# Fp32 operands in place of fp16 pairs in the gate products and the filter's second product of a Hyena/RG-LRU block

## The chip, the cores and the metric

The kernel runs on one core of a Trainium2 chip. The metric is the device time of one execution in microseconds (us). The five engines each work through their own instruction stream in order: PE (TensorE, matrix products; its weight loads are shown apart as PEld), DVE (VectorE), ACT (ScalarE), POOL (GpSimd) and SP (SyncE, which issues DMAs). An instruction that waits holds up everything behind it on its engine.

## The reference, cut to what matters

One block of a hybrid backbone over 4096 tokens of width 1024: normalise and modulate, one input projection into 3072 columns, then two groups side by side. The Hyena group is a long convolution by a filter that a small network computes. The RG-LRU group is a bidirectional recurrence with two gates:

```python
def rglru_coeffs(xc, wa, ba, wx, bx, lam):        # wa, wx: 8 heads of 64x64
    r = sigmoid(einsum('blhi,hij->blhj', xh, wa) + ba)     # xh: xc by heads
    i = sigmoid(einsum('blhi,hij->blhj', xh, wx) + bx)
    log_a = -RG_C * r * softplus(-lam)
    a = exp(log_a)
    b = sqrt(-expm1(2.0 * log_a)) * (i * xc)
    return a, b                                  # h[t] = a[t] * h[t-1] + b[t]

def hyena_filter(L, ...):                        # sines of two-layer products, then
    h = (h @ f_w4) * exp(-t * deltas)            # a 64-row product and a decay
    ...                                          # normalised, forward and backward half
def long_conv(u, kernel, bias):
    y = irfft(rfft(u, n=2 * L) * rfft(kernel, n=2 * L), n=2 * L)[:, :L]
```

The outputs of both groups are normalised, gated, joined, projected by `w_out`, added to x and normalised. 256 context tokens go through the projection and the recurrence first; their last states start the recurrence over the 4096 tokens.

## The kernel before, in words

**Precision.** Almost every product is taken as three products of fp16 operands: an fp32 operand is scaled by a power of two, rounded to fp16 (the high half), and the rest is rounded again (the low half); high·high, high·low and low·high are added up in PSUM in fp32. The helpers `mm` and `mms` issue a matmul; every matmul of the trace is recorded on their line, L168. `pow2` and `total` (L175 to L193) work out the power of two from a sum of squares.

**Stages.** From 0 to about 100 us the modulation vectors are formed and the first weights and tokens come in. From 100 to 200 us the context tokens go through (`ctx_in`, L706), while the filter's network (`mlp`) runs. From 200 to about 900 us pass A (`pass_a`, L579) takes 8 blocks i of 512 tokens. For each it runs 12 projections (`inproj`, 24 fp16 matmuls of 128x512 each; weights in tiles named wh and wz, tokens in X), the short convolutions and the forward recurrence of that block (`units_a`, L855, which calls `unit`, L804, with two lanes for each of two pairs of feature blocks). In between go the 64 rows of the filter (`filter_row`, L967, four to a `filter_group`), and the load of the next block's tokens: two additions on POOL per 128 tokens (xt), squares and copies on ACT, a split into halves (xh on ACT, xlo on POOL), transposing DMAs. From 900 to about 1800 us pass B (`blocks_b`, L1024) goes over the blocks backward: the other projections, the backward recurrence (`units_b`, L1092), the FFT stages, the gating. The rest is the inverse transforms and the output projection.

**A unit of the recurrence** (`unit`, L804) is a generator in steps. Step 1 splits xc (128 x 1024, fp32, two feature blocks side by side) into two fp16 halves in the tile xh: a DVE multiplication by a scale (L810) and a DVE multiply-subtract (L811). Step 2: for each lane and each of two gates three fp16 matmuls (L823) into a PSUM tile of 128x512, fa for gate R and fb for gate I, two buffers each, and a sigmoid on ACT from it (L824). Then POOL multiplies I by xc (L460). Step 3: tanh and exp on ACT (L832, L835), a square on POOL. Step 4: DVE (L841), square root on ACT (L842). Step 5: DVE multiplies (L844), the DVE scans (L849) and carry copies (L851). ACT changes its function table (ACT_TABLE_LOAD) when a function of another set comes next: sigmoid, tanh/exp, square root and the filter's exp take turns.

**Preparation of the gates.** `xc_scale` (L744) bounds xc from the weights' sums by some 25 small DVE instructions to get the power of two for the split, with maxima from `xmax` (L401). `gprep` (L767), once for each direction, loads the 128x1024 fp32 gate weights, scales them (L772, DVE), sums squares (L775, ACT), gets the power of two, and splits them into fp16 halves (L778 ACT, L780 DVE).

**A row of the filter** (`filter_row`): a first product (fp16, three matmuls whl x hb into fa), a DVE product with the decay (kd, L975), the split of kd into kh: high half on ACT (L984), low half on POOL (L985); absolute value on ACT (L978) and its sum on POOL (acc, L457). One row later `second` (L989): three fp16 matmuls kh x st1 into fb, a split of the result on ACT (L995) and DVE (L996), and its store. The decay is an exp on ACT (L963), four in advance in the tile dec.

**What sets the order.** The streams are fixed when the program is built, in order of issue in a tile scheduler with priorities. `mms` lets "side" products (gates, filter, FFT) be placed up to SIDE = 64 instructions earlier than they are written, so they stand in among the projections' matmuls. Steps are hung on a counter by `at` and `tick` (L561 to L568), one tick per projection; the tables DC, DA, DS, D0 give each unit's steps their delays (context, pass A, pass B, last block of pass B). PSUM: mm 3 buffers, fa 2, fb 2, sm 1. fa and fb are shared by the gates, the filter and the FFT, and a matmul into a buffer waits until its former contents were read.

Of the kernel before, what the change touches and what calls it, by code (L numbers as in the profile page):

```python
# [28 lines left out]
DC = (1, 2, 4, 5, 5)  # L29
# [29 lines left out]
DA = ((11, 12, 14, 15, 15), (3, 4, 4, 6, 6), (0, 3, 5, 6, 8))  # L59
# [16 lines left out]
def tables():  # L76
# [35 lines left out]
    t["t_s1"] = np.stack([np.concatenate([hi[:64], hi[:64]]), np.concatenate([lo[:64], lo[:64]]), hi, lo])  # L112
# [50 lines left out]
class K:  # L163
# [73 lines left out]
    def consts(self):  # L237
        nc, a, cp = self.nc, self.a, self.cp
        self.ident = cp.tile([128, 128], F32, name="ident")
        nc.scalar.dma_start(self.ident, a["t_id"])  # L240
        self.ones = cp.tile([128, 128], F32, name="ones")
        nc.vector.memset(self.ones, 1.0)
        self.onesb = cp.tile([128, 128], BF16, name="onesb")
        nc.vector.memset(self.onesb, 1.0)
        self.col = cp.tile([128, 110], F32, name="col")
        self.sT = cp.tile([128, 2, 8], F32, name="sT")
        self.usq = cp.tile([128, NB, 8], F32, name="usq")
        self.shl = cp.tile([128, 2, 8, 2], F16, name="shl")
        self.smax = cp.tile([128, 2], F32, name="smax")
# [67 lines left out]
    def mod(self, pool, ml, xp, part):  # L317
# [42 lines left out]
        if part == 1:  # L360
            junk = pool.tile([128, D], F32, name="gr", bufs=1)
            self.s1, self.sx, self.rsx = s1, *self.xscale(junk, s1, 0)
            self.at(1, lambda: self.xmax(junk, 0))
            return
# [35 lines left out]

    def xmax(self, sq, which):  # L401
        self.nc.vector.tensor_reduce(self.smax[:, which:which + 1], sq, axis=AX.X, op=OP.max)
# [176 lines left out]
    def pass_a(self):  # L579
        tc, nc, a = self.tc, self.nc, self.a  # L580
        with ExitStack() as es, ExitStack() as right:
# [69 lines left out]
            for d in (0, 1, 2, 4):  # L651
                self.at(CT + d, lambda: next(ctx))
# [56 lines left out]
    def ctx_in(self, ap, hy, W):  # L709
# [10 lines left out]
        self.xmax(sq, 1)  # L720
        self.xc_scale(rn, W)
        self.gh, self.rg = [None, None], [None, None]
        self.gprep(0, rn)
        yield
# [19 lines left out]
    def xc_scale(self, pool, W):  # L744

        nc = self.nc
        B = pool.tile([128, NB], F32, name="xb0")
        E = pool.tile([128, NB], F32, name="xb1")
        G = pool.tile([128, 16], F32, name="xb2")
        m = pool.tile([128, 1], F32, name="xb3")  # L750
        for j in range(NB):
            nc.vector.tensor_copy(B[:, j:j + 1], W["xr", j][4])
            be = W["xr", j][2]
            nc.vector.tensor_mul(G[:, 0:2], be, be)
            nc.vector.tensor_reduce(E[:, j:j + 1], G[:, 0:2], axis=AX.X, op=OP.add)
        nc.vector.tensor_reduce(m, self.smax, axis=AX.X, op=OP.max)
        nc.vector.tensor_scalar(m, m, 1.01 * D, None, op0=OP.mult)
        nc.vector.scalar_tensor_tensor(B, B, m, E, op0=OP.mult, op1=OP.add)
        nc.vector.tensor_mul(G, self.col[:, 48:64], self.col[:, 48:64])
        nc.vector.tensor_reduce(E, G.rearrange("p (k j) -> p j k", k=4), axis=AX.X, op=OP.add)  # L760
        nc.vector.scalar_tensor_tensor(B, B, 16.0, E, op0=OP.mult, op1=OP.mult)
        nc.vector.tensor_mul(E, self.col[:, 64:68], self.col[:, 64:68])
        nc.vector.scalar_tensor_tensor(B, E, 2.0, B, op0=OP.mult, op1=OP.add)
        nc.vector.tensor_reduce(m, B, axis=AX.X, op=OP.add)
        self.sxr, self.rxr = self.pow2(self.cp, m, 15, 0, "xr", 1)

    def gprep(self, d, pool):  # L767

        nc, a = self.nc, self.a
        gw = self.wp.tile([128, NB, 2, 128], F32, name="wr", bufs=1)  # L770
        nc.sync.dma_start(gw, a["rg_w"][d])
        nc.vector.tensor_scalar(gw, gw, self.rxr, None, op0=OP.mult)  # L772
        gh = pool.tile([128, 2, NB, 2, 128], F16, name=f"gh{d}")
        gq = pool.tile([128, 1], F32, name=f"gq{d}")
        nc.scalar.activation(gh[:, 0], gw, AF.Square, accum_out=gq)  # L775
        t = self.total(pool, self.ps, gq, "g")
        sg, self.rg[d] = self.pow2(pool, t, 15, 0, f"g{d}", 1)
        nc.scalar.activation(gh[:, 0], gw, AF.Copy, scale=sg)  # L778
        f = lambda t: t.rearrange("p j g c -> p (j g c)")
        nc.vector.scalar_tensor_tensor(f(gh[:, 1]), f(gw), sg, f(gh[:, 0]), op0=OP.mult, op1=OP.subtract)  # L780
        self.gh[d] = gh
# [22 lines left out]
    def unit(self, pool, lanes, n, xc, fin, sig=None):  # L804
# [4 lines left out]
        xh = pool.tile([128, 2052], F16, name="xh", bufs=2)  # L809
        nc.vector.tensor_scalar(xh[:, :2 * n], x2, self.sxr, None, op0=OP.mult)  # L810
        nc.vector.scalar_tensor_tensor(xh[:, 1026:1026 + 2 * n], x2, self.sxr, xh[:, :2 * n], op0=OP.mult,  # L811
                                       op1=OP.subtract)
        yield
        R = pool.tile([128, 1026], F32, name="R", bufs=2)
        I = pool.tile([128, 1026], F32, name="I", bufs=2)
        for l, (d, j) in enumerate(lanes):
            for g, dst, bias in ((0, R, 68 + 4 * d + j), (1, I, 76 + 4 * d + j)):
                for q0 in range(0, n, 512):
                    m = min(512, n - q0)
                    c = n * (j % 2) + q0  # L820
                    ps = self.pst("fa" if g == 0 else "fb", 2)
                    for k, (gi, xi) in enumerate(((0, 0), (0, 1), (1, 0))):
                        self.mms(ps[:, :m], self.gh[d][:, gi, j, g, :], xh[:, 1026 * xi + c:1026 * xi + c + m], k == 0, k == 2)  # L823
                    nc.scalar.activation(dst[:, n * l + q0:n * l + q0 + m], ps[:, :m], AF.Sigmoid,  # L824
                                         bias=self.ccol(bias), scale=self.rg[d])
# [12 lines left out]
        M = xh.bitcast(F32)[:, :L * n]  # L838
# [76 lines left out]
    def filter_setup(self, pool):  # L915
        tc, nc, a = self.tc, self.nc, self.a
        self.st1 = pool.tile([128, 256], F16, name="st1")
        nc.scalar.dma_start(self.st1.rearrange("p (h m) -> p h m", h=2), a["t_s1"][2:4].rearrange("h p m -> p h m"))
# [48 lines left out]
    def filter_row(self, pool, n, hb, dec):  # L967
# [6 lines left out]
        kd = pool.tile([128, 512], F32, name="kd", bufs=1)  # L974
# [8 lines left out]
        kh = pool.tile([128, 2, 512], F16, name="kh", bufs=2)  # L983
        nc.scalar.activation(kh[:, 0], kd, AF.Copy)  # L984
        nc.gpsimd.tensor_sub(kh[:, 1], kd, kh[:, 0])  # L985
# [3 lines left out]
        def second():  # L989
            ps = self.pst("fb", 2)  # L990
            for x, (ti, ki) in enumerate(((0, 0), (0, 1), (1, 0))):
                self.mms(ps, self.st1[:, 128 * ti:128 * ti + 128], kh[:, ki, :], x == 0, x == 2)
# [10 lines left out]
    def filter_l1(self, pool, kd):  # L1003
# [10 lines left out]
        br = pool.tile([1, 512], F32, name="kh", bufs=2)  # L1014
# [77 lines left out]
    def units_b(self, rn, i):  # L1092
# [14 lines left out]
        def sig(p):  # L1107
# [4 lines left out]
            return f  # L1112
        us = zip(*[self.unit(rn, [(1, 2 * p), (1, 2 * p + 1)], 512, xcs[p],
                             lambda h, p=p: self.padd(hfs[p], hfs[p], h[:, :1024]), sig(p) if i else None)
                   for p in range(2)])
        for _ in range(4):
# [434 lines left out]
```

## Time and profile before

| | us |
|---|---|
| median of 3 runs (2275.33, 2286.58, 2288.28) | 2286.58 |
| the profiled execution's own time | 2286.44 |
| its span in the trace | 2284.6 |
| PE busy in it | 1920.0 |
| DVE busy | 1498.6 |
| ACT busy | 1151.6 |
| POOL busy | 862.5 |

Spans and busy times come from the one profiled execution. A busy PE includes the pipelined ends of its matmuls: a 128x512 fp16 matmul is recorded with 0.38 us, while the next begins 0.21 us after it. So the distance from start to start is what a matmul adds to the stream. The mean granted clock of TensorE over the execution was 0.927.

### The profile page before, as it was taken

To read this page: it belongs to the slowest core of one execution; us is meant where nothing else is said; L and a number is where in the kernel's file an instruction comes from. 1 tells how busy PE (TensorE), PEld (TensorE's weight loads), DVE (VectorE), ACT (ScalarE), POOL (GpSimd) and SP (SyncE) were. 2 spreads that over 40 slices of the span, in tenths; PEclk is the share of its full clock that TensorE was granted. 3 is DMA by queue.
4 is the path that set the end of the run, shared out by engine and by line. 5 is a ranking of instruction groups with operands and counts; after the bars stand their busy time and mean duration, and the time that the engine had idled before them with its cause. 6 is when DMAs were issued, how large, how long until landed. Compare 5 with 4: busy or idle time off the path is not lost. (4 is left out here: it accounts for less than half of the span.)

```text
span 2284.6 us, 30912 instructions
## 1 busy us (share of the span) xinstructions
PE 1920.0 (84%) x10858; PEld 919.7 (40%) x10858; DVE 1498.6 (66%) x2871; ACT 1151.6 (50%) x1803; POOL 862.5 (38%) x571
## 2 busy tenths in 40 slices
PE   6967769989797889878888999797897766999987
PEld 2434324334343334433334555454544433444433
DVE  4895876857576677664644664755756645777776
ACT  3655766665646577575563633645444412422222
POOL 3024655554656453131322443534433321333330
PEclk9988979989898999999899999998998887999999
DMA  9546244435453322566646999899997799454531
GB/s 291 172 115 168 77 137 137 154 81 162 138 150 96 112 87 96 179 196 207 208 143 210 205 217 249 200 227 244 221 257 206 189 270 230 136 163 155 168 120 74
DMA packets 397608, 391.13 MB, mean 171 GB/s; under 512 B 209513, under 2 KB 295935, under 8 KB 392846
## 3 DMA queue, kind: packets, MB, share of 16 engines
q1 hardware_dynamic: 376988, 342.25, 54.2%
q10 hardware_dynamic: 20466, 46.93, 7.2%
q8 instruction: 85, 1.39, 0.3%
q14 instruction: 69, 0.57, 0.1%
HBM read 213.96 MB, written 132.13 MB: 151 GB/s over the span
## 5 line engine op out<-in xcount | busy, mean ns | idle before, releaser
L168 PE MATMUL mm<-X,wh 128*128 128x512 f16 x3072 | 745.8, 389 | 35.4 <-DMA X<-xh 7.5
L168 PEld LDWEIGHTS <-wh 128*128 128x128 f16 x3648 | 326.5, 100 | 466.9 <-issue 102.3
L168 PE MATMUL mm<-X,wz 128*128 128x512 f16 x1536 | 384.8, 395 | 7.5 <-ACT zh L1064 4.5
L168 PEld LDWEIGHTS <-wz 128*128 128x128 f16 x1728 | 159.9, 101 | 226.7 <-issue 58.0
L168 PEld LDWEIGHTS <-hl 128*128 128x128 f16 x1536 | 151.8, 101 | 212.2 <-issue 20.8
L168 PE MATMUL mm<-wz,hl 128*128 128x512 f16 x768 | 181.8, 395 | 18.9 <-DVE hl L1465 13.4
L168 PE MATMUL mm<-X,hl 128*128 128x512 f16 x768 | 179.9, 389 | 7.7 <-DVE wh L1479 5.3
L985 POOL TENSOR_TENSOR kh<-kd,kh 128x512 f16<-128x512 f32 x64 | 84.5, 1321 | 157.4 <-ACT kh L984 157.4
L460 POOL TENSOR_TENSOR I<-I,xc 128x1024 f32<-128x1024 f32 (+3 forms) x36 | 84.1, 2340 | 128.8 <-ACT I L824 114.8
L1241 POOL TENSOR_TENSOR A<-A,B 128x256 f32<-128x256 f32 x64 | 51.0, 797 | 205.9 <-DVE B L1240 187.8
L452 POOL TENSOR_TENSOR xlo<-xt,xh 128x1024 f16<-128x1024 f32 x32 | 76.8, 2414 | 135.8 <-ACT xh L450 135.8
L168 PE MATMUL fb<-tb,vki 128*128 128x128 f16 x768 | 98.1, 225 | 20.6 <-DMA tb<-in_t_s 19.7
L168 PE MATMUL fa<-xh,gh 128*128 128x512 f16 (+3 forms) x228 | 67.4, 396 | 52.2 <-ACT R L824 42.8
L460 POOL TENSOR_TENSOR zr<-zr,sg 128x1024 f32<-128x1024 f32 x16 | 39.1, 2443 | 176.1 <-ACT sg L1110 176.1
L460 POOL TENSOR_TENSOR xh<-R 128x1024 f32<-128x1024 f32 (+2 forms) x34 | 69.4, 2044 | 79.2 <-ACT R L835 77.7
L1252 DVE SCALAR_TENSOR_TENSOR yy<-A,yy 128x512 f16<-128x512 f32 x64 | 57.7, 902 | 62.1 <-ACT yy L1251 62.0
L841 DVE SCALAR_TENSOR_TENSOR xc<-xh,xc 128x1024 f32<-128x1024 f32 (+2 forms) x34 | 58.2, 1714 | 60.7 <-POOL xh L460 60.3
L168 PE MATMUL fa<-tb,vu 128*128 128x128 f16 x768 | 97.0, 225 | 0.0
L457 POOL TENSOR_TENSOR acc<-acc,dec 128x512 f32<-128x512 f32 x64 | 93.7, 1464 | 4.9 <-ACT dec L978 4.9
L849 DVE TENSOR_TENSOR_SCAN I<-R,car,I 128x512 f32<-128x512 f32 (+2 forms) x64 | 94.6, 1502 | 0.1
L168 PEld LDWEIGHTS <-gh 128*128 128x128 f16 x456 | 46.7, 105 | 111.6 <-issue 70.5
L168 PEld LDWEIGHTS <-vki 128*128 128x128 f16 x768 | 76.7, 100 | 33.7 <-issue 24.5
(377 smaller groups left out, 3723.4 us busy)
## 6 DMA issues: line engine op xcount, KB each, us to landing
VkD<-vk SPq DMA_DIRECT2D x64, 256.0 KB, 2.0
VuD<-vo SPq DMA_DIRECT2D x64, 256.0 KB, 2.5
X<-XD SPq DMA_DIRECT2D x8, 2048.0 KB
vu<-VuD SPq DMA_DIRECT2D x128, 128.0 KB, 3.3
vki<-VkD SPq DMA_DIRECT2D x128, 128.0 KB, 3.6
ZD<-zo SPq DMA_DIRECT2D x64, 256.0 KB, 4.3
xt<-in_x SPq DMA_DIRECT2D x30, 512.0 KB, 5.1
XD<-X SPq DMA_DIRECT2D x6, 2048.0 KB
```

The lines of the kernel that those rows point to most:

```text
L168: self.nc.tensor.matmul(out, lhsT, rhs, start=start, stop=stop)
L452: nc.gpsimd.tensor_sub(xl, xt, xh)
L457: self.nc.gpsimd.tensor_add(out, x, y)
L460: self.nc.gpsimd.tensor_mul(out, x, y)
L841: nc.vector.scalar_tensor_tensor(Z, M, 1.0, Z, op0=OP.add, op1=OP.mult)
L849: nc.vector.tensor_tensor_scan(f(h), f(r), f(h), 0.0 if c is None else c, op0=OP.mult, op1=OP.add)
L985: nc.gpsimd.tensor_sub(kh[:, 1], kd, kh[:, 0])
L1241: nc.gpsimd.tensor_sub(A[:, :, 0, :], A[:, :, 0, :], B[:, :, 1, :])
L1252: nc.vector.scalar_tensor_tensor(yy[:, :, 1, :], yv, 0.125, yy[:, :, 0, :], op0=OP.mult, op1=OP.subtract)
```

## The change

The gates take xc and their weights as they are, in fp32: one matmul per product in place of three. The scaled split of xc, the bound xc_scale with xmax, and the scaling and splitting of the gate weights are gone; `gprep` only loads. The steps of `unit` are one fewer; the tables DC and DA lose the entry of that step (the first one of each triple in DA), the context's entry 4 becomes 3, and pass B yields once without work where the split stood. The filter's second product takes kd in fp32 with an fp32 table; the split of kd on ACT and POOL is gone, and kd has three buffers in place of one. The tile that took xh's place for the square in step 3 is now allocated by itself.

```diff
-DC = (1, 2, 4, 5, 5)
+DC = (1, 3, 4, 4)
-DA = ((11, 12, 14, 15, 15), (3, 4, 4, 6, 6), (0, 3, 5, 6, 8))
+DA = ((12, 14, 15, 15), (4, 4, 6, 6), (3, 5, 6, 8))
...
-            for d in (0, 1, 2, 4):
+            for d in (0, 2, 4):
                 self.at(CT + d, lambda: next(ctx))
...
-        self.xmax(sq, 1)
-        self.xc_scale(rn, W)
-        self.gh, self.rg = [None, None], [None, None]
+        self.gw = [None, None]
         self.gprep(0, rn)
-        yield
         self.gprep(1, self.wp)
...
     def gprep(self, d, pool):
-        gw = self.wp.tile([128, NB, 2, 128], F32, name="wr", bufs=1)
-        nc.sync.dma_start(gw, a["rg_w"][d])
-        nc.vector.tensor_scalar(gw, gw, self.rxr, None, op0=OP.mult)
-        gh = pool.tile([128, 2, NB, 2, 128], F16, name=f"gh{d}")
...
-        nc.scalar.activation(gh[:, 0], gw, AF.Square, accum_out=gq)
...
-        nc.scalar.activation(gh[:, 0], gw, AF.Copy, scale=sg)
...
+        self.gw[d] = pool.tile([128, NB, 2, 128], F32, name=f"gw{d}")
+        self.nc.sync.dma_start(self.gw[d], self.a["rg_w"][d])
...
         x2 = xc[:, :2 * n]
-        xh = pool.tile([128, 2052], F16, name="xh", bufs=2)
-        nc.vector.tensor_scalar(xh[:, :2 * n], x2, self.sxr, None, op0=OP.mult)
-        nc.vector.scalar_tensor_tensor(xh[:, 1026:1026 + 2 * n], x2, self.sxr, xh[:, :2 * n], op0=OP.mult,
-                                       op1=OP.subtract)
-        yield
...
-                    for k, (gi, xi) in enumerate(((0, 0), (0, 1), (1, 0))):
-                        self.mms(ps[:, :m], self.gh[d][:, gi, j, g, :], xh[:, 1026 * xi + c:1026 * xi + c + m], k == 0, k == 2)
-                    nc.scalar.activation(dst[:, n * l + q0:n * l + q0 + m], ps[:, :m], AF.Sigmoid,
-                                         bias=self.ccol(bias), scale=self.rg[d])
+                    self.mms(ps[:, :m], self.gw[d][:, j, g, :], x2[:, c:c + m], True, True)
+                    nc.scalar.activation(dst[:, n * l + q0:n * l + q0 + m], ps[:, :m], AF.Sigmoid, bias=self.ccol(bias))
...
-        M = xh.bitcast(F32)[:, :L * n]
+        M = pool.tile([128, 1026], F32, name="xh", bufs=2)[:, :L * n]
...
-        kd = pool.tile([128, 512], F32, name="kd", bufs=1)
+        kd = pool.tile([128, 512], F32, name="kd", bufs=3)
...
-        kh = pool.tile([128, 2, 512], F16, name="kh", bufs=2)
-        nc.scalar.activation(kh[:, 0], kd, AF.Copy)
-        nc.gpsimd.tensor_sub(kh[:, 1], kd, kh[:, 0])
...
-            for x, (ti, ki) in enumerate(((0, 0), (0, 1), (1, 0))):
-                self.mms(ps, self.st1[:, 128 * ti:128 * ti + 128], kh[:, ki, :], x == 0, x == 2)
+            self.mms(ps, self.st1, kd, True, True)
```

On PE, in a burst of gate products of pass A, among the projections' matmuls (mm<-X,wz), the stream of before reads as follows; gh is a half of the gate weights, xh a half of xc:

```order
L168 MATMUL mm<-X,wz 128x512
L168 LDWEIGHTS gh_1506
L168 MATMUL fa<-xh,gh_1506 128x512
L168 LDWEIGHTS wz
L168 MATMUL mm<-X,wz 128x512
L168 LDWEIGHTS gh_1506
L168 MATMUL fa<-xh,gh_1506 128x512
L168 LDWEIGHTS gh_1506
L168 MATMUL fa<-xh,gh_1506 128x512
L168 LDWEIGHTS gh_1506
L168 MATMUL fb<-xh,gh_1506 128x512
```

And at the corresponding place of the changed program, where gw are the fp32 gate weights (a matmul of fp32 operands brings its weight load with it, so it has no row of its own here):

```order
L169 MATMUL mm<-X,wz 128x512
L169 MATMUL fa<-xc,gw_1531 128x512
L169 LDWEIGHTS wz
L169 MATMUL mm<-X,wz 128x512
L169 MATMUL fb<-xc,gw_1531 128x512
L169 LDWEIGHTS wz
L169 MATMUL mm<-X,wz 128x512
L169 MATMUL fa<-xc,gw_1531 128x512
```

One product between two projections' matmuls stands where three stood, and the second buffer of a tag is asked for after fewer matmuls.

On ACT, the sigmoids of the first pass-A burst that stands beside a filter group, before:

```order
L824 ACT_TABLE_LOAD
L824 ACTIVATE R<-fa,col,p2r_g_1519 128x512
L824 ACTIVATE I<-fb,col,p2r_g_1519 128x512
L824 ACTIVATE R<-fa,col,p2r_g_1519 128x512
L824 ACTIVATE I<-fb,col,p2r_g_1519 128x512
...
L963 ACT_TABLE_LOAD
L963 ACTIVATE dec<-dl,dcol 128x512 x4
```

and after (L777 is the sigmoid, L915 the filter's exp there):

```order
L777 ACT_TABLE_LOAD
L777 ACTIVATE R<-fa,col 128x512
L777 ACTIVATE I<-fb,col 128x512
L777 ACTIVATE R<-fa,col 128x512
L915 ACT_TABLE_LOAD
L915 ACTIVATE dec<-dl,dcol 128x512
L777 ACT_TABLE_LOAD
L777 ACTIVATE I<-fb,col 128x512
```

One of the four exp of the filter group now stands in the middle of the burst, with a table load ahead of it and one behind. Over the whole program ACT has 67 table loads before and 80 after.

On DVE, in pass B, ahead of the sum q1r from which the scale of a block's gated recurrence output is formed (xc<-xcD had been loaded for the next block's unit), the stream before:

```order
L1127 TENSOR_TENSOR zr<-zr,hf 128x1024 x2
L810 TENSOR_SCALAR xh<-xc,p2s_xr 128x1024 x2
L811 SCALAR_TENSOR_TENSOR xh<-xc,p2s_xr,xh 128x1024 x2
L1151 TENSOR_REDUCE q1r<-qs 128x1
L189 CAST p2b_yr<-q1r 128x1
```

and after:

```order
L803 COPY car_15350<-I 128x1
L1076 TENSOR_TENSOR zr<-zr,hf 128x1024
L1100 TENSOR_REDUCE q1r<-qs 128x1
L190 CAST p2b_yr<-q1r 128x1
L194 COPY p2t_yr<-sm 128x1
```

The four instructions of the split between the last product zr and the sum are gone.

## Rows read from the trace of the kernel before

**Rows 1.** The page's part 1: engine, busy us, share of the span, instructions.

```profile
PE   1920.0 (84%) x10858; PEld 919.7 (40%) x10858; DVE 1498.6 (66%) x2871; ACT 1151.6 (50%) x1803; POOL 862.5 (38%) x571
```

**Rows 2.** Busy us of pass A; columns PE, PEld, DVE, ACT, POOL, clock, DMA share, GB/s.

```profile
200.00:900.00 700.00, 591.16 (x2702) 258.18 (x2700) 481.04 (x831) 448.57 (x758) 377.94 (x237) 0.91 0.41 122
```

**Rows 3.** The same columns for the first half of the context's stretch.

```profile
100.00:150.00 50.00, 39.15 (x274) 20.16 (x273) 49.22 (x165) 26.90 (x44) 8.23 (x4) 0.93 0.38 96
```

**Rows 4.** Timeline of PE: start, duration (us), instruction; an fp32 product and its follower.

```profile
92.01 1.02 PE L168 MATMUL fb<-x,bm 128*128 128x512 f32 x2
92.87 1.46 PE L168 MATMUL mm<-X,wh 128*128 128x512 f16 x6
```

**Rows 5.** Timeline of PE: two gate products of three fp16 matmuls each.

```profile
276.00 0.81 PE L168 MATMUL fa<-xh,gh 128*128 128x512 f16 x3
276.64 0.81 PE L168 MATMUL fb<-xh,gh 128*128 128x512 f16 x3
```

**Rows 6.** Groups on PE by shape: count, busy us, mean ns, idle before.

```profile
L168 PE MATMUL fb<-kh,st 128*128 128x512 f16 x192 | 61.1, 392 | 15.4 <-DVE vk L996 11.0 <-POOL kh L985 4.4
L168 PE MATMUL fa<-xh,gh 128*128 128x512 f16 x180 | 58.4, 417 | 44.1 <-ACT R L824 34.7 <-DVE kd L975 8.0 <-DVE vo L1201 1.0
```

**Rows 7.** PE's waits over the run: us in total, times, longest.

```profile
PE fa L168 <- ACT R L824: 43.2, 10, 14.5
```

**Rows 8.** PE's waits from 200 to 900 us.

```profile
PE fa L168 <- ACT R L824: 33.6, 7, 14.5
PE fb L168 <- DVE car L851: 14.0, 1, 14.0
PE fa L168 <- DVE kd L975: 11.0, 5, 3.6
```

**Rows 9.** Groups on DVE by shape: the split of xc, and the scans.

```profile
L811 DVE SCALAR_TENSOR_TENSOR xh<-xc,p2s_xr,xh 128x1024 f16<-128x1024 f32 x28 | 44.2, 1584 | 0.4
L810 DVE TENSOR_SCALAR xh<-xc,p2s_xr 128x1024 f16<-128x1024 f32 x28 | 28.2, 1013 | 10.3 <-DMA xc<-xcD 10.1
```

**Rows 10.** Groups on ACT by shape: sigmoids, the split of kd, table loads.

```profile
L824 ACT ACTIVATE R<-fa,col,p2r_g 128x512 f32<-128x512 f32 x60 | 46.3, 777 | 7.7 <-PE fa L168 7.0
L984 ACT ACTIVATE kh<-kd 128x512 f16<-128x512 f32 x64 | 40.1, 627 | 77.6 <-DVE kd L975 73.6 <-DVE xc L525 2.2 <-DVE cvx L525 1.4
L824 ACT ACT_TABLE_LOAD x10 | 12.8, 1283 | 1.8 <-DVE I L849 1.6
```

**Rows 11.** Groups on POOL by shape.

```profile
L985 POOL TENSOR_TENSOR kh<-kd,kh 128x512 f16<-128x512 f32 x64 | 84.5, 1321 | 157.4 <-ACT kh L984 157.4
```

**Rows 12.** DVE's gate weights by line (min/median/max ns, starts); timeline, a small instruction.

```profile
L772 DVE TENSOR_SCALAR wr<-wr,p2r_xr x2: 748/1678/2609, 138.8 to 156.2; 128x1024 f32<-128x1024 f32 x2
L780 DVE SCALAR_TENSOR_TENSOR gh<-wr,p2s_g,gh x2: 1273/1779/2285, 147.2 to 162.3; 128x1024 f16<-128x1024 f32 x2
...
131.26 0.16 DVE L761 SCALAR_TENSOR_TENSOR xb<-xb,xb 128x4 f32<-128x4 f32 x1
```

**Rows 13.** Timeline, a long wait of PE near 291 us; bracket: idle before, releaser.

```profile
291.46 0.59 PE L168 MATMUL fb<-xh,gh 128*128 128x512 f16 x1 [14.01 <-DVE car L851]
...
292.12 1.44 PE L168 MATMUL fa<-xh,gh 128*128 128x512 f16 x3
```

**Rows 14.** Timeline, a long wait of PE near 695 us, and what ran ahead.

```profile
685.05 1.15 POOL L985 TENSOR_TENSOR kh<-kd,kh 128x512 f16<-128x512 f32 x1
...
687.46 2.56 ACT L963 ACTIVATE dec<-dl,dcol 128x512 f32<-128x512 f32 x4 [8.54 <-POOL acc L457]
...
694.90 1.44 PE L168 MATMUL fa<-xh,gh 128*128 128x512 f16 x3 [14.47 <-ACT R L824]
```

**Rows 15.** Timeline, a wait of PE in pass B, and DVE ahead of it.

```profile
1734.76 2.42 DVE L810 TENSOR_SCALAR xh<-xc,p2s_xr 128x1024 f16<-128x1024 f32 x2
...
1737.10 4.48 DVE L811 SCALAR_TENSOR_TENSOR xh<-xc,p2s_xr,xh 128x1024 f16<-128x1024 f32 x2
...
1741.89 0.16 PE L168 MATMUL sm<-p2b_yr,onesb 128*128 128x1 bf16 x1 [8.28 <-DVE p2b_yr L189]
```

More of the change, by code (lines that the diff above doesn't have):

```diff
@@ L111, in tables @@
     hi, lo = split16(t1)
-    t["t_s1"] = np.stack([np.concatenate([hi[:64], hi[:64]]), np.concatenate([lo[:64], lo[:64]]), hi, lo])
+    t["t_s1"] = np.stack([np.concatenate([hi[:64], hi[:64]]), np.concatenate([lo[:64], lo[:64]])])
+    t["t_s1f"] = t1.astype(f32)
     fw_ = np.zeros((64, 128, 128))
@@ L248, in consts @@
         self.shl = cp.tile([128, 2, 8, 2], F16, name="shl")
-        self.smax = cp.tile([128, 2], F32, name="smax")
         self.kp = cp.tile([128, 8], F32, name="kp")
@@ L362, in mod @@
             self.s1, self.sx, self.rsx = s1, *self.xscale(junk, s1, 0)
-            self.at(1, lambda: self.xmax(junk, 0))
             return
@@ L399, in xscale @@
         return f, rsx
-    def xmax(self, sq, which):
-        self.nc.vector.tensor_reduce(self.smax[:, which:which + 1], sq, axis=AX.X, op=OP.max)
     def xload(self, pool, src, pos, xts=None, rp=None, lag=0):
@@ L741, in ctx_in @@
         yield
[L744 to L765, printed above, removed]
-    def gprep(self, d, pool):
-        nc, a = self.nc, self.a
-        gw = self.wp.tile([128, NB, 2, 128], F32, name="wr", bufs=1)
-        nc.sync.dma_start(gw, a["rg_w"][d])
-        nc.vector.tensor_scalar(gw, gw, self.rxr, None, op0=OP.mult)
-        gh = pool.tile([128, 2, NB, 2, 128], F16, name=f"gh{d}")
-        gq = pool.tile([128, 1], F32, name=f"gq{d}")
-        nc.scalar.activation(gh[:, 0], gw, AF.Square, accum_out=gq)
-        t = self.total(pool, self.ps, gq, "g")
-        sg, self.rg[d] = self.pow2(pool, t, 15, 0, f"g{d}", 1)
-        nc.scalar.activation(gh[:, 0], gw, AF.Copy, scale=sg)
-        f = lambda t: t.rearrange("p j g c -> p (j g c)")
-        nc.vector.scalar_tensor_tensor(f(gh[:, 1]), f(gw), sg, f(gh[:, 0]), op0=OP.mult, op1=OP.subtract)
-        self.gh[d] = gh
+    def gprep(self, d, pool):
+        self.gw[d] = pool.tile([128, NB, 2, 128], F32, name=f"gw{d}")
+        self.nc.sync.dma_start(self.gw[d], self.a["rg_w"][d])
     def rnn_consts(self, pool):
@@ L916, in filter_setup @@
         tc, nc, a = self.tc, self.nc, self.a
-        self.st1 = pool.tile([128, 256], F16, name="st1")
-        nc.scalar.dma_start(self.st1.rearrange("p (h m) -> p h m", h=2), a["t_s1"][2:4].rearrange("h p m -> p h m"))
+        self.st1 = pool.tile([128, 128], F32, name="st1")
+        nc.scalar.dma_start(self.st1, a["t_s1f"])
         self.dl = pool.tile([128, 512], F32, name="dl")
@@ L1013, in filter_l1 @@
         self.mm(ps[0:1, :], self.ones[:, 0:1], self.acc, True, True)
-        br = pool.tile([1, 512], F32, name="kh", bufs=2)
+        br = pool.tile([1, 512], F32, name="br", bufs=1)
         nc.scalar.dma_start(br, self.a["hy_bias"])
@@ L1112, in sig @@
             return f
+        yield
         us = zip(*[self.unit(rn, [(1, 2 * p), (1, 2 * p + 1)], 512, xcs[p],
@@ L1115, in units_b @@
                    for p in range(2)])
-        for _ in range(4):
+        for _ in range(3):
             next(us)
```

## The prediction

> **What bounds the kernel now.** The page's part 1 comes first: PE is the busiest engine, DVE the next [rows 1]. The busy times of pass A then show that no engine is full there: PE has 109 of 700 us without work [rows 2]. So a microsecond added to PE's stream is a microsecond of time only where PE does not wait next, and a microsecond taken from DVE, ACT or POOL is worth something only where PE waits for them. The exception is the first half of the context's stretch, in which DVE is busy for 49.22 of 50 us and bounds everything [rows 3]. PE's waits say where it stands: over the run ten times for the sigmoid that empties fa, 43.2 us [rows 7]; in pass A 33.6 us of that, 14.0 us in one wait that the trace puts down to the carry copy, and 11.0 us for kd [rows 8]; and for the filter's second product 11.0 us behind vk and 4.4 us behind kh, which the group of kh x st1 carries in its idle column [rows 6].
>
> **The change, part by part.** The sum is made against the profiled execution, 2286.44 us, which is the median (2286.58) to a tenth of a microsecond.
>
> *PE's stream.* Three fp16 matmuls take 0.64 us, from 276.00 to the next start at 276.64 [rows 5]. The trace of before holds fp32 products of the same shape, those of the filter's network: one is recorded as two matmuls and the next thing starts 0.86 us after it [rows 4]. So a full-width product costs 0.22 us more. There are 192: 64 of the filter (192 matmuls of kh x st1), 60 each for R and I (180 matmuls in the fa group, as many in fb) [rows 6], and 8 of 511 columns for block 0. That is 192 x 0.22 = 42 us, and the 16 context products of 256 columns add half of that each, 2 us: **+44**. At the mean clock of pass A, 0.91 [rows 2], it would be 48, which is the upper bound; the lower is 40, since 0.02 us is the step in which starts are read. About 28 us of it lie in pass A, 14 in pass B, 2 in the context.
>
> *Weight loads.* An fp32 weight load is part of its product; the 0.86 us above held one in steady flow, so nothing is added.
>
> *Bursts that already wait for ACT.* Where the fifth product of a burst waits for the first sigmoid, the four products ahead of it (two buffers of fa, two of fb) can each be 0.22 us longer and the wait just shrinks. Ten such waits [rows 7], 10 x 4 x 0.22 = **-9**. Bounds: -4 (half of them too short or fed by PE) and -18 (all eight products covered). A sigmoid takes 0.777 us [rows 10], less than the fp32 product, so the second four are paced by PE and get nothing.
>
> *Table loads.* The order shows 80 for 67; 13 x 1.283 us [rows 10] = 17 us more on ACT, against 40.1 us that go with the split of kd. Where the added pair stands inside a burst, it delays the next sigmoid by 0.71 + 2 x 1.28 = 3.3 us, but two buffers and the projections between cover most: **+3**, bounds 0 and +17.
>
> *The start.* Removed from DVE: scaling and splitting of both gate weights, 0.75 + 2.61 + 1.27 + 2.29 = 6.9 us [rows 12]; the context's two splits at half width, 2 x (1.01 + 1.58) / 2 = 2.6 us [rows 9]; and about 36 instructions on a few columns at 0.16 us [rows 12], 5.8 us: 15 us in all. In a stretch where DVE is 98% busy [rows 3] this should come back, but the context's projections, transposes and the filter's network must also be ready; I take some seven tenths, **-11**, bounds 0 and -15.
>
> *Pass A, the filter's chain.* kd to kh on ACT (64 x 0.627 us) and POOL (64 x 1.321 us, the larger) [rows 10, 11] leaves the path of the second product, and kd gets three buffers. PE's waits behind vk, kd and kh are 26.4 us together [rows 6, 8]. The 4.4 go; of the others a third to a half, since the row's own DVE product and the fb buffers remain: **-13**, bounds -4 and -26.
>
> *Pass A, DVE.* The long wait at 291 us ends when DVE has done a row of scans [rows 13]; what stood ahead of it on DVE includes the next unit's split, of the size of two times (1.01 + 1.58) us [rows 9]. So half of the 14.0 goes: **-7**, bounds 0 and -14. The wait at 695 us is ACT's: ACT was held 8.54 us by the sum acc on POOL, which came behind kh and acc in turn; with kh gone, four times 1.15 us leave that queue [rows 14]. Of pass A's waits for the sigmoid, 33.6 less 6 already counted, I take a quarter: **-7**, bounds -3 and -20.
>
> *Pass B, DVE.* The split of the next unit stands right ahead of the sum that a scale needs: from 1734.76 to 1741.5 us DVE does nothing else, and PE waits 8.28 us for what follows [rows 15]. 6.8 us go there, and 2.2 at one other place: **-9**. Bounds: -3, as the added 14 us of PE may arrive where nothing waits, and -20, as 40 us less of DVE [rows 9] may also shorten other waits. What is late next at this place is the load of the block's stored states.
>
> *Clock.* Behind a long wait PE runs at the lower level: three gate matmuls are recorded with 1.44 us after the wait at 291 [rows 13], 0.81 at the full one [rows 5]. A wait that is gone spares such a tail of 2 us; two or three of them, **-4**, bounds 0 and -8.
>
> *The sum:* 44 - 9 + 3 - 11 - 13 - 7 - 7 - 9 - 4 = -13, so **2273 us**. The unknown ends taken together would give -81 and +51, but they will not all fall one way.
>
> **A rule that bears on it.** The trace shows DVE's split of 128x1024 at 1.58 us on average [rows 9] and at 2.24 us in the place above [rows 15]; the rows do not show by what. The Trainium skill, "SBUF — State Buffer", section "Terms", says that DVE and GpSimd share a port pair, held for a whole instruction, and that the loser is fully blocked. By that rule taking 84.5 us of POOL work away gives DVE back whatever its two-input instructions waited in it, and the DVE terms would stand at their large bounds: a sum of about -44 (-26 for the filter's chain, -14 for the scans, -20 for pass B, the other terms as they are). No row here shows whose instruction waited for the port, so I count only the named waits.
>
> **The rivals.** *Slower.* PE is the bound and the products are simply longer. The mechanism is the stream of PE in pass A and B: +44, with the ten bursts' cover -9, and every other wait of PE kept, since its releaser sits elsewhere: the waits for transposes, for FFT results and for the loads are not touched. If of the give-backs of 51 us less than 15 come true, the time is over 2309. I put this case at 2286 + 44 - 9 + 3 - 10 = 2314 us, and it decides wherever the waits moved instead of shrinking. For it speaks PE's 84% [rows 1]; against it, that DVE's 98% in the start is plain [rows 3]. Chance 0.22.
>
> *Faster.* Pass A is not bound by PE but by the chain of token load, sigmoids, recurrence and filter on the other three engines, and PE's waits there are its signs. That chain loses 84.5 us of POOL [rows 11], 40 of ACT [rows 10] and some 41 of DVE, while PE's 109 idle us [rows 2] absorb its 28. If a third of the idle time goes beyond the absorbed, pass A gets shorter by some 20 to 25 us, the start by 11, pass B by 4: about 2250 us. For it: the two longest waits in pass A are behind such work [rows 13, 14]. Against: POOL is busy for 378 of 700 us in pass A [rows 2], so its queue is long only at times. Chance 0.36.
>
> *Cheaper products.* If an fp32 product of this shape ran at twice the rate that the trace shows, it would take 0.43 us in place of 0.64, the stream would lose 40 us where it gains 44, and the time would be about 2273 - 84 = 2189 us. The row with 0.86 [rows 4] speaks against it; the operands there are a network's weights and activations of the same shape. Chance 0.02. The rule is that of the Trainium skill, "Perfetto Trace Analysis", section "Engine Utilization", whose note gives half the output rate for fp32 taken as low and high; the trace of before does not agree with it.
>
> **How the numbers follow.** Forecast, a change within 1% (23 us, about what a measurement of this kernel tells from none): 2273 us, chance 0.40, own range 2260 to 2300. Faster by over 1%: the chain and the cheap product, 0.36 + 0.02 = 0.38. Slower by over 1%: 0.22. The range leaves about a tenth out on each side: down to 2236, past the middle of the faster case, and up to 2314, the middle of the slower one.
>
> **What would show it.** In the profile after: fp32 gate products 0.86 us from start to start beside projections; PE's busy time up by some 50 us or more (its records overlap); the waits behind kh gone and those behind vk smaller; the long waits at 291 and 695 us shorter by 7 and 3 to 5 us; the context's stretch shorter by about 11 us with DVE still full in it; the wait for p2b_yr at 1742 us down to 1 or 2 us; pass B's length within 5 us. I am wrong if pass A's waits return under other names (the x-load's DMA, the exp in the middle of a burst), if the fp32 products keep the lower clock longer and cost 1.7 us there, or if the start is bound by what DVE waits for rather than by DVE.

## The result and the profile after

| | before | after |
|---|---|---|
| median, us | 2284.51 (4 runs, 2275.33 to 2288.28) | 2258.6 (4 runs, 2257.68 to 2266.64) |
| span of the profiled execution, us | 2284.6 | 2257.4 |
| mean granted clock of TensorE in it | 0.927 | 0.947 |

The ratio is 0.9897, with a 95% interval of 0.9871 to 0.9923: 24 us by the ratio, 26 by the medians, or 1.0% faster. The forecast was 2273 us within 2236 to 2314, so the time lies inside the range, and the gain is about twice the 13 us of the sum. It lies on the border between "within 1%" and "faster by over 1%".

The page's part 1 and its row of the granted clock in 40 slices, after:

```profile
PE 1933.1 (86%) x10640; PEld 931.0 (41%) x10640; DVE 1395.2 (62%) x2763; ACT 1122.5 (50%) x1746; POOL 769.7 (34%) x507
...
PEclk9988999999999999999999999999999998999999
```

Against [rows 1] DVE lost 103 us, POOL 93 and ACT 29, and PE gained 13 in its records, which overlap. Busy times of the two passes, after (PE, PEld, DVE, ACT, POOL, clock, DMA share, GB/s):

```profile
200.00:900.00 700.00, 627.08 (x2688) 277.25 (x2688) 457.48 (x854) 435.49 (x720) 289.93 (x172) 0.95 0.44 126
900.00:1800.00 900.00, 774.48 (x4860) 397.17 (x4859) 489.95 (x799) 463.01 (x672) 305.12 (x216) 0.95 0.79 210
```

In pass A PE's idle time went from 109 to 73 us, and its clock from 0.91 to 0.95 [rows 2]. Pass B kept its length. To see where the time went I matched the projections' matmuls, which both programs issue in one sequence, and read when the first one of a block starts:

| first projection matmul of | before, us | after, us | difference |
|---|---|---|---|
| pass A, second block | 206.32 | 205.90 | -0.4 |
| pass A, third block | 335.39 | 313.41 | -22.0 |
| pass A, fourth block | 421.28 | 410.22 | -11.1 |
| pass B | 917.10 | 894.80 | -22.3 |
| pass B, about a third through | 1230.27 | 1203.97 | -26.3 |
| pass B, about three quarters through | 1626.43 | 1615.15 | -11.3 |
| pass B, the last one | 1852.35 | 1826.58 | -25.8 |

So the start gave nothing, the second block of pass A gave 22 us of which half went again, pass A as a whole gave 22, the middle of pass B lost 15, and its end brought them back. These are single executions, one of each kernel. PE's waits from 200 to 900 us, after (us in total, times, longest):

```profile
PE mm L169 <- DMA X<-xh: 18.3, 3, 9.0
PE fa L169 <- DVE kd L927: 15.1, 5, 9.2
PE fa L169 <- ACT R L777: 14.3, 3, 7.0
PE mm L169 <- DMA X<-xlo: 12.1, 5, 6.4
```

The waits for the sigmoid fell from 33.6 to 14.3 us, those for the carry copy, vk and kh are gone [rows 6, 8], and kd's went from 11.0 to 15.1. The waits for the next block's tokens, X<-xh and X<-xlo, now lead with 30.4 us; before, they were 14.0:

```profile
PE mm L168 <- DMA X<-xh: 7.5, 2, 4.9
PE mm L168 <- DMA X<-xlo: 6.5, 4, 2.8
```

### The profile page after: what moved, and what is told of

Read it like the earlier page. It is cut to its first block, busy times and chain, and to the rows that moved or that the text cites. A ratio compares the mean times of both kernels' runs of the same rounds, so it can differ in the third digit from the quotient of the medians.

```text
span 2257.4 us, 30208 instructions
## 1 busy us (share of the span) xinstructions
PE 1933.1 (86%) x10640; PEld 931.0 (41%) x10640; DVE 1395.2 (62%) x2763; ACT 1122.5 (50%) x1746; POOL 769.7 (34%) x507
## 5 line engine op out<-in xcount | busy, mean ns | idle before, releaser
L169 PE MATMUL mm<-X,wz 128*128 128x512 f16 x1536 | 370.4, 387 | 3.4 <-ACT zh L1012 3.4
L453 POOL TENSOR_TENSOR acc<-acc,dec 128x512 f32<-128x512 f32 x64 | 88.0, 1375 | 194.8 <-ACT dec L930 187.0
L169 PE MATMUL fa<-xc,gw 128*128 128x512 f32 (+3 forms) x152 | 79.8, 615 | 38.1 <-ACT R L777 20.8
L1188 DVE TENSOR_TENSOR A<-fa,kf 128x512 f32<-128x512 f32 x64 | 43.9, 686 | 78.1 <-ACT kf L1184 72.3
L1150 DVE TENSOR_TENSOR vo<-fa,vo 128x512 f16<-128x512 f32 x64 | 43.1, 688 | 72.9 <-ACT vo L1149 72.5
L1200 ACT ACTIVATE yy<-A 128x512 f16<-128x512 f32 x64 | 40.1, 626 | 87.6 <-POOL A L1191 56.5
```

The costliest lines, as they stand in the source:

```text
L169: self.nc.tensor.matmul(out, lhsT, rhs, start=start, stop=stop)
L453: self.nc.gpsimd.tensor_add(out, x, y)
L1150: nc.vector.tensor_sub(vo[:, :, 1, :], pv, vo[:, :, 0, :])
L1188: nc.vector.tensor_mul(A, u4, kf[:, :, 0:1, :].to_broadcast([128, NB, 2, 64]))
L1200: nc.scalar.activation(yy[:, :, 0, :], yv, AF.Copy, scale=0.125)
```

## The experiments

Theory A, that of the forecast: the gain is work taken off DVE, ACT and POOL; PE's longer stream is partly absorbed. Rivals: B, the longer products themselves keep the clock up; C, PE is the bound and its stream counts in full. Every kernel is laid out anew by the scheduler, so instructions away from an edit move too; I read nothing into differences under about 5 us. All of them were timed beside runs of the kernel before, whose medians were 2277 to 2282 us from one set to the next; so kernels of different sets are compared by their ratios to it, and 0.01 of ratio is 23 us.

**The longer stream alone, and the removed work alone.** Upon the kernel before, in the gates and in the same way in the filter's second product:

```diff
-                    for k, (gi, xi) in enumerate(((0, 0), (0, 1), (1, 0))):
+                    for k, (gi, xi) in enumerate(((0, 0), (0, 1), (1, 0), (1, 1))):
...
```

> The kernel before with the low x low term added as a fourth fp16 matmul to every gate product and every second filter product: PE's stream gets about as much longer as by the fp32 products (208 products, about 0.21 us each, 42 us), and nothing is taken from any other engine. Theory A (the gain comes from the work taken off DVE, ACT and POOL; PE's longer stream is partly absorbed by waits): 15 to 30 us slower than before, granted clock within 0.01 of before's 0.927. Theory B (the longer products themselves keep the clock up, and the removed work matters little): no slower than before, clock 0.94 or more. Theory C (PE is the bound, every microsecond of stream counts): 42 to 46 us slower.

Upon the changed kernel, in the gates and in the same way in the filter's second product:

```diff
+def top(t):
+    return t.bitcast(BF16).rearrange("p (c h) -> p c h", h=2)[:, :, 1]
...
-                    self.mms(ps[:, :m], self.gw[d][:, j, g, :], x2[:, c:c + m], True, True)
+                    for k in range(3):
+                        self.mms(ps[:, :m], top(self.gw[d][:, j, g, :]), top(x2[:, c:c + m]), k == 0, k == 2)
...
```

> The changed kernel with each fp32 product replaced by three matmuls that read the upper 16 bits of the fp32 operands as bf16 (less precise, so the output differs): all of the removed work stays removed, but PE's stream is as short as before. Theory A: 25 to 40 us faster than the changed kernel (2220 to 2235 us), clock as high as after's 0.945, which would then come from the shorter waits. Theory B: the clock falls back to about 0.93 and the time is within 10 us of before (2275 to 2290). Theory C: 42 us faster than the changed kernel (2216 us).

Measured: the fourth product made it slower, ratio 1.0102 (1.0078 to 1.0126), 23 us; the bf16 kernel was faster, 2237.2 us, ratio 0.9811 (0.9786 to 0.9836), 43 us against before and, from 0.9897, 20 against the changed kernel. So the longer products cost 20 to 23 us in either surrounding, half of the 42 us that they add to the stream. The first lies in theory A's range, the second misses it by 2 us (2237.2 against 2220 to 2235); C, with the full length, falls. But the length is not all that differs in these pairs, since ACT's order changes with PE's. The changed kernel has 80 table loads, the bf16 kernel 70, which is 13 us of ACT; the fourth product has 72 where the kernel before has 67. The sigmoids' part of it, changed kernel and then bf16 kernel:

```profile
L777 ACT ACT_TABLE_LOAD x17 | 21.8, 1283 | 2.0 <-issue 1.7
```

```profile
L782 ACT ACT_TABLE_LOAD x13 | 16.7, 1283 | 2.3 <-issue 2.1
```

How much of the 20 to 23 us is the length and how much are the table loads, no run here parts. The removed work alone, with the bf16 kernel's order, is worth 43 us. The clock of the profiled executions:

```profile
core 0: 2309.6 us, clock 0.932
```

```profile
core 0: 2234.0 us, clock 0.939
```

The first is the fourth product's, the second the bf16 kernel's. Over their runs it was 0.932 to 0.935 and 0.934 to 0.939; before, in the runs made beside them, 0.924 to 0.931, and after 0.942 to 0.947. Both raise it. B is right that a longer stream goes with a slightly higher clock, but it does not make the kernel faster.

**Each half of the change.** The edits are the diff's own, the filter's part or the gates' part alone.

> Only the filter's half of the change (fp32 second product, no split of kd, three buffers of kd; the bias row takes its place in a vk buffer). By the steps of the prediction: +14 of stream, -13 for the filter's chain, -3 to -7 for the sigmoids behind POOL's queue: 2 to 6 us faster than before. Rival: the filter's split on POOL and ACT paces pass A, and then this half alone brings 15 us or more.

> Only the gates' half of the change (fp32 gate products, no split of xc, no scale bound, no split of the gate weights, tables as in the changed kernel). By the steps: +30 of stream, -9 of covered bursts, -7 at 291 us, -9 in pass B, nothing in the start (where after shows the gain lost to a wait for the next tokens), -4 of clock: within 5 us of before. Rival: the gates' half carries the gain, 15 us or more faster, and with the filter's half near nothing.

Measured: the filter's half 2255.7 us, ratio 0.9886 (0.9867 to 0.9905), 26 us faster; the gates' half 2280.6 us, ratio 0.9997 (0.9981 to 1.0013). The filter's half is the whole gain, over four times the most that my steps gave it (2 to 6 us), so the rival of the third expectation holds; the gates' half came out as its steps had it. PE's waits from 200 to 900 us with the filter's half:

```profile
PE fa L169 <- DVE kd L976: 19.1, 4, 10.8
PE fa L169 <- ACT R L825: 18.7, 7, 7.3
PE mm L169 <- DMA X<-xh: 12.3, 3, 4.5
```

and with the gates' half:

```profile
PE mm L168 <- DMA X<-xh: 25.8, 5, 9.0
PE fa L168 <- DVE kd L926: 17.9, 6, 5.6
PE fa L168 <- ACT R L776: 17.1, 3, 9.1
```

Both halves shorten the sigmoids' waits. But with the gates' half the longest wait is for the next tokens, whose two additions and low half go through POOL; with the filter's half that wait is half as long.

**Which engine's queue.** Upon the filter's half the work that it removed was put back as dead work, so that nobody waits for its result, on POOL (with the second line below, the next experiment) or on ACT (with the third, the one after it):

```diff
+        scr = pool.tile([128, 512], F16, name="scr", bufs=1)
+        nc.gpsimd.tensor_sub(scr, kd, self.whl[:, 0])
+        nc.scalar.activation(scr, kd, AF.Copy)
```

> The filter's half alone (2256 us), with POOL's subtraction put back as dead work: 64 times kd minus an fp16 tile into a tile that nobody reads, at the place of the old split. POOL has its 84 us again, but the second product does not wait for it. Theory A1 (POOL's queue was what the filter's split cost: tokens' additions, acc and I x xc stood behind it): 15 to 25 us of the 26 are lost, 2271 to 2281 us. Theory A2 (the chain kd, ACT, POOL, second product and the single kd were what it cost): 2254 to 2262 us.

> The filter's half alone (2256 us), with ACT's copy of kd put back as dead work: 64 copies of 0.63 us into a tile that nobody reads. If ACT's queue is what paced pass A (sigmoids, squares and splits of the tokens behind it): 2265 us or more, and the waits for the sigmoid back from 18.7 to about 30 us. If it was POOL's queue or the chain: 2254 to 2260 us.

Measured: with POOL's work back 2277.4 us, ratio 0.9979 (0.9964 to 0.9994), so some 21 of the 26 us are lost. With ACT's copy back 2263.4 us, ratio 0.9919 (0.9891 to 0.9947), some 8 us lost, between the two ranges that were expected and with an interval that touches that of the filter's half. So A2 falls: what the split of kd cost was mainly its work on POOL, not the chain to the second product. The projections' matmuls show where. From the second block of pass A to the start of pass B the kernel before takes 710.8 us, the filter's half 685.4, the gates' half 702.9, the filter's half with POOL's work back 708.1, with ACT's copy back 697.0; pass B takes 925 to 937 us in every kernel. The group of the dead work on POOL, and ACT's wait for POOL's sum in pass A:

```profile
L985 POOL TENSOR_TENSOR scr<-kd,whl 128x512 f16<-128x512 f32 x64 | 84.9, 1326 | 148.4 <-DVE kd L976 104.3 <-DVE xc L526 12.7 <-DVE cvv L526 8.5
```

```profile
ACT dec L964 <- POOL acc L458: 26.8, 11, 6.7
```

That wait was 21.0 us in 8 times with the filter's half alone:

```profile
ACT dec L964 <- POOL acc L458: 21.0, 8, 7.9
```

One way in which POOL's work costs time is seen at one place. Before, PE waits 14.47 us for a sigmoid, ACT had been held 8.54 us by the sum acc, which stood behind kh on POOL [rows 14]. The same place in the changed kernel:

```profile
667.16 1.27 POOL L453 TENSOR_TENSOR acc<-acc,dec 128x512 f32<-128x512 f32 x1 [2.24 <-ACT dec L930]
...
668.46 2.56 ACT L915 ACTIVATE dec<-dl,dcol 128x512 f32<-128x512 f32 x4 [1.44 <-POOL acc L453]
...
675.99 2.08 PE L169 MATMUL fa<-xc,gw 128*128 128x512 f32 x2 [6.96 <-ACT R L777]
```

POOL now waits for ACT, ACT is held 1.44 us, and PE 6.96. POOL is busy for only 290 to 380 of 700 us in pass A in these kernels; at this place a queue that is half empty on the mean still held up the next engine. How much of the 21 us comes this way is not shown: ACT's wait above differs by 5.8 us.

A rival of the queue is left, which the prediction raised under "A rule that bears on it": POOL's work may make DVE's instructions longer. The totals go that way. Part 1 of the page of the filter's half alone, and of the same with POOL's work back:

```profile
PE 1918.7 (85%) x10794; PEld 922.6 (41%) x10794; DVE 1484.9 (66%) x2871; ACT 1121.2 (50%) x1739; POOL 779.3 (35%) x507
```

```profile
PE 1927.0 (85%) x10794; PEld 923.2 (41%) x10794; DVE 1493.5 (66%) x2871; ACT 1118.7 (49%) x1739; POOL 863.7 (38%) x571
```

The same 2871 instructions of DVE take 8.6 us longer; with ACT's copy back they take 1483.0 us. A1 asks for POOL's queue, and the runs show POOL's work: its place ahead of other POOL instructions and its effect on DVE are not parted.

**The start.** One number upon the changed kernel, so that the convolution of pass A's first block and the tokens' split go ahead of the context's sigmoids on ACT, as before:

```diff
-DC = (1, 3, 4, 4)
+DC = (2, 3, 4, 4)
```

> The changed kernel with one number changed: the first delay of the context's unit 2 in place of 1, so that ACT has the convolution of block 0 (and with it the split of the next tokens) ahead of the context's sigmoids again, as before the change. If the start's gain was lost there (the changed kernel waits 9.0 and 6.4 us for the next block's tokens): block 1 starts some 6 us earlier and the time is 2250 to 2254 us. If the transposes or the loads of the tokens are late by themselves: no change, 2256 to 2262 us, with the wait for X<-xh in place.

Measured: 2258.2 us, ratio 0.9897 (0.9869 to 0.9924), no change. The waits for the tokens did shrink, from these of the changed kernel

```profile
205.90 1.44 PE L169 MATMUL mm<-X,wh 128*128 128x512 f16 x3 [9.00 <-DMA X<-xh]
213.69 2.74 PE L169 MATMUL mm<-X,wh 128*128 128x512 f16 x6 [6.36 <-DMA X<-xlo]
```

to these,

```profile
206.56 0.81 PE L169 MATMUL mm<-X,wh 128*128 128x512 f16 x3 [2.30 <-DMA X<-xh]
207.77 10.10 PE L169 MATMUL mm<-X,wh 128*128 128x512 f16 x46 [0.40 <-DMA X<-xlo]
```

but the second block starts at 206 us all the same, since PE now waits earlier, 6.05 us for the context's first sigmoid. The kernel before waits for the same tokens at the same time:

```profile
206.32 1.44 PE L168 MATMUL mm<-X,wh 128*128 128x512 f16 x3 [2.62 <-DMA X<-xh]
```

I had taken the order of ACT's stream for the cause; it is not the only one. In all three kernels the second block starts when X<-xh has landed, whatever PE waited for earlier. Why the tokens land at 206 us in each is open.

**The halves without their longer products.** The same bf16 views, upon the gates' half and upon the filter's half:

> The gates' half alone (2281 us), with its fp32 products replaced by three bf16 matmuls on the upper 16 bits (less precise output): the gates' removed work without the longer stream. If the gates' half gives 15 us by the removed work and loses them by 28 us of stream: 2262 to 2268 us. If the removed work of the gates is worth nothing: 2278 to 2284 us.

> The filter's half alone with its fp32 product replaced by three bf16 matmuls on the upper 16 bits (less precise output): the filter's removed work without 14 us of stream. If PE's stream costs half of its length once POOL is relieved: 2246 to 2251 us. If it costs all: 2242. If pass A's waits absorb it: 2253 to 2257.

Measured: gates 2276.2 us, ratio 0.9980 (0.9963 to 0.9996); filter 2252.0 us, ratio 0.9885 (0.9864 to 0.9905). So alone the gates' removed work is worth 5 us and the filter's 26; together they are worth 43 (the bf16 kernel above). Upon the filter's half, then, the gates' removed work is worth 17. That it pays only where POOL is relieved is a reading, not shown by itself: the difference of 12 us comes from three ratios, and by their intervals it is uncertain by some 8 us to either side. The longer products, by the same ratios: the filter's cost nothing that can be told (0.9886 against 0.9885), the gates' 4 us alone (0.9997 against 0.9980, intervals that overlap), and both together 20. The table loads go the same way: 67 with and without the filter's longer product, 76 against 70 with the gates', 80 against 70 with both. Of the three expected sizes of the filter's product the last fits the ratios, that the waits absorb it; 2252.0 us itself lies just under its range. One place where PE waits longer beside the gates' longer products is plain in its waits over the whole run. After:

```profile
PE fb L169 <- ACT kf L1184: 14.2, 10, 3.6
```

With the gates' half and bf16 products:

```profile
PE fb L172 <- ACT kf L1192: 1.3, 4, 0.6
```

It was 0.7 us before, 8.9 with the fourth product, 17.4 with the gates' half alone. These are FFT products of pass B that wait for a buffer of fb, which they share with the gates. Whether it is the length of the gates' products or the order that the scheduler makes of it, these runs do not tell.

**A step further.** If POOL's work paces pass A, the other POOL work of a filter row should go too: its sum of absolute values, to DVE.

```diff
             nc.scalar.activation(dec, kd, AF.Abs)
-            self.padd(self.acc, self.acc, dec)
+            nc.vector.tensor_add(self.acc, self.acc, dec)
```

> The changed kernel with the other POOL work of a filter row taken away too: the sum acc of absolute values is added on DVE (64 x about 0.7 us) in place of POOL (64 x 1.4 us). Theory A1 (pass A is paced by POOL's queue): pass A's waits for the sigmoid shrink again and the time is 2235 to 2250 us. Rival: after the change POOL's queue no longer ends any long wait, PE and DVE do: 2253 to 2265 us.

> The same move of the sum to DVE, upon the filter's half alone (2256 us; gates as before). DVE is fuller here by the split of xc. Theory A1: 2235 to 2250 us. Rival: DVE is the next engine in pass A, and its 45 us more cost what POOL's 88 us less bring: 2252 to 2262 us.

Measured: upon the changed kernel 2247.3 us, ratio 0.9871 (0.9846 to 0.9895), against its 0.9897 some 6 us faster, which the intervals do not part. Upon the filter's half 2234.0 us, ratio 0.9813 (0.9791 to 0.9834): 17 us faster than that half and 43 faster than before, faster than both kernels, and it keeps the fp16 gates. Its pass A:

```profile
200.00:900.00 700.00, 632.80 (x2902) 280.57 (x2901) 528.48 (x977) 448.88 (x741) 214.51 (x112) 0.96 0.44 133
```

and the sum on DVE, beside the sum on POOL in the changed kernel:

```profile
L980 DVE TENSOR_TENSOR acc<-acc,dec 128x512 f32<-128x512 f32 x64 | 55.3, 864 | 16.6 <-ACT dec L979 16.2
```

```profile
L453 POOL TENSOR_TENSOR acc<-acc,dec 128x512 f32<-128x512 f32 x64 | 88.0, 1375 | 194.8 <-ACT dec L930 187.0 <-ACT R L777 7.7
```

DVE is now busy for 528 of 700 us and POOL for 215. Over the execution DVE is busy for 1513.7 us, 26 less than the filter's half's 1484.9 and the sum's 55.3 together, so here too DVE's other work became shorter as POOL's went. That POOL's work paces pass A holds on the filter's half, and only weakly on the whole change: upon this kernel the gates' half costs 13 us (2247.3 against 2234.0, one set), and it has 80 table loads there against 69.

## Why the prediction was right or wrong, point by point

- **PE's stream, +44:** right in size for the stream. A full-width fp32 product takes 0.86 us at the full clock, and at the lower level 1.71, from 477.39 to 479.10 in the first fence and from 482.70 to 483.56 in the second:

```profile
477.39 1.91 PE L169 MATMUL fb<-xc,gw 128*128 128x512 f32 x2
479.10 0.64 PE L169 MATMUL mm<-X,wz 128*128 128x512 f16 x1
```

```profile
482.70 1.02 PE L169 MATMUL fb<-kd,st 128*128 128x512 f32 x2
483.56 0.81 PE L169 MATMUL mm<-X,wz 128*128 128x512 f16 x3
```

  What the longer products cost in time, table loads included, was measured at 20 to 23 us. The prediction covered 9 of the 44 in the bursts; the true cover was over twice that. The sign "PE's busy time up by some 50 us or more" failed: it rose by 13.
- **Cheaper products:** out, by the same rows: 0.86 us where twice the rate would be 0.43. The note of the Trainium skill, "Perfetto Trace Analysis", section "Engine Utilization", gives half the output rate for FP32_LOW_HIGH. Taken for the whole product, as the prediction takes it, the trace does not agree; but the product is recorded as two matmuls (x2 above), 0.43 us each in the 0.86, and half of the fp16 matmul's rate fits each of them.
- **Table loads, +3:** the 13 more came. They go with the gates' longer products: 76 to 80 with these in fp32, 67 to 70 with bf16 or with the gates as before and no fourth product. Their price lies somewhere in the 20 us between the changed and the bf16 kernel and is not parted from the stream; nothing here shows that it is as small as 3. But the sigmoids became shorter, which I did not see coming (last section).
- **The start, -11:** wrong. DVE's busy time in it did fall, and the context's gates came 6 us earlier, but the second block starts at 205.90 us where it started at 206.32. The step that failed is "this should come back": the next block's tokens land at 206 us either way, and moving ACT's order did not bring it either. Here the prediction's own sign of being wrong came true, a wait that returns under the name of the x-load's DMA: 9.00 us for X<-xh and 6.36 for X<-xlo.
- **The filter's chain, -13, and a quarter of the sigmoids' waits, -7:** the mechanism for the first was wrong and the second too small. The filter's half brings 26 us net of its own stream of 14, and 21 of them hang on POOL's work. I had priced the chain to the second product and named POOL's queue only at 695 us, for which I took a quarter of the sigmoids' waits; that wait alone went from 14.47 to 6.96 us, where 3 to 5 were forecast. The rival "faster" described it ("the chain of token load, sigmoids, recurrence and filter") and gave 2250 us.
- **The rule on DVE and POOL:** its sum of -44 was not reached, and the -13 that counts the named waits alone was too small. DVE's same instructions did become shorter as POOL's work went, 1498.6 to 1484.9 us with the filter's half, so it may be behind a part of that half's 26 us. No run here sets it against the queue.
- **DVE at 291 us, -7:** the wait of 14.0 us is gone and the third block starts 22 us earlier, but each half alone does that (16.6 and 20.9 us there), so it looks like one stall that either removes, not two gains. With bf16 products upon the gates' half it is only 5.5 us, and after the whole change the next block gives half of it back; these are single traces.
- **Pass B, DVE, -9:** wrong. The wait for p2b_yr that was 8.28 us [rows 15] is 8.10 after:

```profile
1714.63 2.27 DVE L1076 TENSOR_TENSOR zr<-zr,hf 128x1024 f32<-128x1024 f32 x1 [0.94 <-POOL hf L453]
...
1717.89 1.04 ACT L1084 ACTIVATE sg<-zr 128x1024 f32<-128x1024 f32 x1
...
1719.06 0.15 DVE L1100 TENSOR_REDUCE q1r<-qs 128x1 f32<-128x2 f32 x1 [2.16 <-ACT sg L1084]
...
1719.45 0.16 PE L169 MATMUL sm<-p2b_yr,onesb 128*128 128x1 bf16 x1 [8.10 <-DVE p2b_yr L190]
```

  With the split gone, the sum q1r waits for ACT's squares, which wait for DVE's zr and POOL's hf. The split had run beside that chain. I had named what is late next as a load; it was this, and it takes all of the wait. It is the wait that took the place of the one removed.
- **Clock, -4:** right in kind; what it is worth in us no run tells. The mean went from 0.927 to 0.947, in pass A from 0.91 to 0.95. That shorter waits did all of it is not so: the bf16 kernel, with the same work removed, shows 0.934 to 0.939, so a part of the rise seems to go with the longer products, as with the fourth product.
- **The chances:** the median lies at 1.0%, between my forecast and the faster rival, to which the mechanism belongs: POOL's work in pass A. That the sum came out near is luck: terms that were too large (start, pass B) and terms too small (POOL's work, the cover) went against each other.

## What to carry to other kernels

The busiest engine is not always the one whose work is worth removing. POOL was busy half of the time in pass A, and at one place it held ACT, and ACT held PE; 85 us of work put back on POOL cost 21 us, where as much off DVE (the split of xc, 84.5 us in all, with the rest of the gates' preparation) was worth 5 alone and 17 upon the filter's half. Before a saving is credited to the wait that it stands in, follow the waiting instruction's other inputs; if they are ready no earlier, the wait stays under another name. A change of two halves is to be measured in halves: here one carried all of it, and the fastest kernel here, which also moves the sum to DVE, keeps the other half undone. A longer product can also change the order on another engine: count its table loads before the difference is put down to the length.

## What the runs showed of the hardware that was not expected

The sigmoids of the gates became shorter by 93 ns. Before they took 777 ns [rows 10]; after, without the scale that was read from a column of SBUF:

```profile
L777 ACT ACTIVATE R<-fa,col 128x512 f32<-128x512 f32 x60 | 40.9, 684 | 7.7 <-PE fa L169 7.3
```

With the filter's half alone, which keeps the scale, it is 777 again:

```profile
L825 ACT ACTIVATE R<-fa,col,p2r_g 128x512 f32<-128x512 f32 x60 | 46.4, 777 | 10.1 <-PE fa L169 10.0
```

The Trainium skill, "ScalarE: Activation LUTs", section "What ACT_TABLE_LOAD costs", states that each pointer operand adds about 93 ns to an activation; the trace agrees, 777 against 684. For 128 full sigmoids that is 12 us of ACT, which stood in no term of the sum.

The 864 ns of the sum on DVE against 1375 on POOL go with the Trainium skill, "GPSIMD Engine Reference", section "3.1 Elementwise — side-by-side cycle accounting", which advises DVE for elementwise work; the ratio here is 1.6, where the page measures 1.96 on a longer row.
